# A two-layer encoder on one core: half of the second attention's probability tiles transposed on VectorE and through DRAM, and the softmax factor multiplied into the gate

## The chip, the core and the metric

The kernel runs on one core of a Trainium2 chip. The core has five engines that run their own instruction lists in order: PE (TensorE, matrix multiplication; the profile lists its weight loads apart, as PEld), DVE (VectorE), ACT (ScalarE), POOL (GpSimd) and SP (SyncE), which here issues all DMAs. Matrix products land in PSUM, eight banks of 128 x 512 floats, and DVE or ACT carries them to SBUF. POOL works on SBUF only. The metric is the device time of one execution in microseconds, and lower is better.

## The reference

The program is two encoder layers over 1024 tokens of width 1024. The first uses differential attention, the second multi-head latent attention; the change is in the second.

```python
def _mla(h, positions, w_in, q_a_norm_g, w_q_b, kv_a_norm_g, w_kv_b, w_out):
    proj = h @ w_in
    q_a, c_kv, k_pe, z = jnp.split(proj, [384, 640, 704], axis=-1)
    q = (_rmsnorm(q_a, q_a_norm_g) @ w_q_b).reshape(b, s, 8, 128 + 64)
    q_nope, q_pe = q[..., :128], _rope(q[..., 128:], positions)
    k_pe = _rope(k_pe[:, :, None, :], positions)[:, :, 0]
    kv = (_rmsnorm(c_kv, kv_a_norm_g) @ w_kv_b).reshape(b, s, 8, 128 + 128)
    k_nope, v = kv[..., :128], kv[..., 128:]
    # for each block of 128 queries
    sc = (einsum('bqhd,bkhd->bhqk', qn, k_nope) + einsum('bqhr,bkr->bhqk', qp, k_pe)) * 192 ** -0.5
    p = jax.nn.softmax(sc, axis=-1)
    o = einsum('bhqk,bkhd->bqhd', p, v)
    return (o.reshape(b, s, 1024) * jax.nn.silu(z)) @ w_out
```

There are eight heads, so the second attention has 8 x 8 = 64 blocks of 128 queries against 1024 keys.

## The kernel before

**Stages.** The program runs the first layer's projections, its attention, its output projection, then the second layer's projections, its attention (`attn1`, L1710, called for heads 0 to 6 at L1780 and for the last head at L1815) and its output projection. All matrix products take each operand as a high part and a low part (what rounding to the `fp32r` form leaves over), and multiply high x high, high x low and low x high (`mm3`, L186 to L188).

**One block of scores.** `scores1` (L1687) makes the scores of 128 queries against 1024 keys, a tile `s` of two PSUM banks, out of ten products of 512 columns (L1703). There are two such tiles (`sc=2`), so the block after next needs the first one's tile back. `softmax_part` (L401) takes the row maximum on DVE (L404) and the exponential on ACT (L406), which reads `s` and writes `e` to SBUF together with the row sum in `zz`. The factor 1/sum is not applied there.

**Transposing.** The second product needs the probabilities with the keys on the partitions. `transpose_p` (L382) does half a block: four transposes of 128 x 128 on PE (L387) into the one bank `tr`, then ACT copies the bank to the high part `pth` (L389), then DVE subtracts that from the bank into the low part `ptl` (L390). The bank is free for the next half when DVE is through. A block has two halves, in `Tail.turn(0)` and `turn(1)`.

**The second product.** Two blocks make a pair. `Tail.pv` (L987) multiplies the pair's `pth` and `ptl` with the head's values `vt` into the bank `pv`: 12 products of 256 columns for each half of the keys, 24 for the pair. Two pairs fill the bank (a half of the 1024 queries). `close` in `attn1` then multiplies the bank with the gate `gz` on DVE (L1721), and `finish` (L910) inverts `zz` (L1722), spreads it over the partitions by a DMA to DRAM and back (`bc_d`, `bc_s`), multiplies it in on POOL (L916), splits the result into high and low (L921, L922) and stores both (`oS`).

**The order.** Python code names the order by hand, and a build step may move an instruction on its own engine where its inputs stand late in that step's plan; what stands then is fixed. For block n, `scores1` issues its ten products with `turn(1)` of block n-2 after the sixth. `after_scores` (L1019) issues `turn(0)` of block n-1, and behind each second block the second product of the pair before. Between these stand steps of a stream of other products, the projections of the next heads' queries and keys (`FILL1`, L42: how many steps at which of four places; one step is three products `acc` of 512 columns). The SP queue issues the DMAs in its own order, and a DMA that waits holds all behind it. The values of a head are two tiles `vt` of 512 KB out of three buffers.

The last head is called with no stream steps, and works on the output projection's first products (`oacc`) instead.

Of the kernel before, what the change touches and what calls it, by code (L numbers as in the profile page):

```python
# [21 lines left out]
P = 128  # L22
D = 1024
# [18 lines left out]
FILL1 = ((1, 0, 1, 0), (0, 1, 0, 0)) * 4  # L42
# [28 lines left out]
HL_V = (0, 1)  # L71
Q_CHUNK = 6
# [19 lines left out]
def trunk(ctx: ExitStack, tc: tile.TileContext, A, out):  # L92
# [303 lines left out]
    def alloc_pt(ap_):  # L396
        pth = [ap_.tile([P, 4, 2 * P], F32R, name="pth", tag="pt", bufs=6) for _ in range(2)]
        ptl = [ap_.tile([P, 4, 2 * P], F32R, name="ptl", tag="pt", bufs=6) for _ in range(2)]
        return pth, ptl
# [510 lines left out]
    def finish(o, y, l, h, half, dst, ap_, dgs):  # L910

        if dst is None:
            b, rb = bcast_rows(ap_, y, "osq", 4)
# [60 lines left out]
    class Tail:  # L974
# [12 lines left out]
        def pv(self, kh):  # L987
            c, qp = self.c, self.qp
            if self.t == 0:
                return  # L990
            if kh == 0:
                if qp == 0:
                    c["vt"] = load_v(c["pool"], c["l"], c["h"])
                if qp % 2 == 0:
                    c["o_"] = bank("pv", "pv")
                    c["open"](qp // 2)
            cs = slice((qp % 2) * 256, (qp % 2) * 256 + 256)
            pv(c["o_"][:, cs], c["vt"], *self.pt, kh)
            if kh == 1 and qp % 2 == 1:
                c["close"](qp // 2, c["o_"], self.zz)  # L1000

    tails, hooks = [None, None], []

# [15 lines left out]
    def after_scores(fill, n):  # L1019

        prev, last = tails
        if last:
            last.turn(0)
        fill(n)
        if prev:
            prev.pv(0)
        fill(n + 1)
        new = hooks[:]
        if prev:
            prev.pv(1)  # L1030
        fill(n + 2)
        for f in new:
            hooks.remove(f)
            f()

    def attn0(h, fills, extra=None, late=None):
# [10 lines left out]
        ctx_ = dict(pool=a0b, l=0, h=h, open=lambda half: None, close=close)  # L1047
        for qp in range(4):
            half = qp // 2
            if qp % 2 == 0:  # L1050
                zz = first.pop(0) if first else sm.tile([P, 4], F32, name="zz")
            for t in range(2):
# [13 lines left out]
                if first:  # L1066
                    e0 = first.pop()
                else:
                    e0 = q_tile(h, half, (qp * 2 + t) % 4, zz, a0b, mid)
                    fill(2)  # L1070
                    after_scores(fill, 3)
                side.tick()
                tails[:] = [tails[1], Tail(qp, t, e0, zz, ctx_)]
# [171 lines left out]
    tail0 = attn0(NH - 1, lambda i: FILL7[i] if i < Z_LAST else (0,) * 6, extra0, late0)  # L1245
    mk.clear()
# [30 lines left out]
    def group0(gi, fulls):  # L1277
# [3 lines left out]
        def chunk(k):  # L1281
            if gi == 1:
                h1[k][1] = xt2k("h1h"), xt2k("h1l")
                h1f[k] = ut(f"h1f{k}", dt=F32)
# [19 lines left out]
    def ut(name, spare=False, dt=F32R):  # L1304
        return up.tile([P, HF], dt, name=name, tag="us" if spare else "u", bufs=4 if spare else 20)
# [4 lines left out]
    wp = pool(stw, "wp1", side="right")  # L1310
    stv = ExitStack()
# [31 lines left out]
    def combos():  # L1343
# [5 lines left out]
        for k in range(4):  # L1349
# [19 lines left out]
            split_t(3, k, t3_, (ut("t3h"), ut("t3l")))  # L1369
# [228 lines left out]
    cqput = lora(3, CQ, qag, QL, lambda: ut("cqr", dt=F32), lambda: ut("cq"), 1)  # L1598
# [4 lines left out]
    def gate_steps():  # L1603
# [14 lines left out]
        for j in range(KT):  # L1618
# [6 lines left out]
            for i in range(2):  # L1625
                with behind("V"):
# [60 lines left out]
    def scores1(h, half, ti, zz):  # L1687
# [18 lines left out]
        return softmax_part(ap, s_ps, zz[:, ti : ti + 1])  # L1706
# [3 lines left out]
    def attn1(h, fills, extra=None, late=None):  # L1710

        def open_(half):
            ctx_["gz"] = wst.tile([P, HF], F32, name="gz1", tag="gz", bufs=3)
            SP.dma_start(ctx_["gz"], zS[h, half])

        def close(half, o_, zz):
            if late and half == 1:
                ctx_["late"] = late(o_, zz, ctx_["gz"])
                return
            o = ap2.tile([P, HF], F32, name="o1", tag="o", bufs=2)  # L1720
            V.scalar_tensor_tensor(out=o, in0=o_, scalar=0.5, in1=ctx_["gz"], op0=ALU.mult, op1=ALU.mult)  # L1721
            V.reciprocal(zz, zz)  # L1722
            finish(o, zz, 1, h, half, None, ap2, None)

        ctx_ = dict(pool=ap, l=1, h=h, open=open_, close=close)
        for qp in range(4):
            half = qp // 2
            if qp % 2 == 0:
                zz = first1.pop(0) if first1 else sm.tile([P, 4], F32, name="zz1")
            for t in range(2):  # L1730
# [7 lines left out]
                if first1:  # L1738
# [207 lines left out]
```

## Time and profile before

| | us |
|---|---|
| median of three runs | 1428.52 (1428.01 to 1430.89) |
| the profiled execution | 1429.47 |
| its span on the core | 1427.7 |
| PE busy in the span | 1396.7 |
| DVE / ACT / POOL busy | 903.3 / 743.3 / 603.7 |
| the stretch 1040 to 1290 us, in the second attention: PE / DVE / ACT / POOL busy | 249.6 / 145.3 / 129.0 / 67.8 of 250 |

The span leaves out 1.8 us of the profiled execution's own time. A row of a group reads: line, engine, operation, out<-in by the program's names, shapes and count, then busy time and mean duration of one in ns, then how long the engine stood idle just before these instructions and what ended it. Products on PE are pipelined: the profile shows one of 512 columns as about 0.39 us long, while the next one starts 0.23 us after it. So a busy share of PE counts overlap once and can't be divided by the mean duration; how long PE needs for a row of products is read from the starts in the timeline.

### The profile page before, as it was taken

Reading aid. Unit: us, or ns where it says so; the run is one execution under the profiler, and the core shown is the slowest. Engines: PE = TensorE matmul, PEld = TensorE weight load, DVE = VectorE, ACT = ScalarE, POOL = GpSimd, SP = SyncE. Lnnn points to the kernel's source line nnn. Section 1 sums busy time; section 2 is a strip of 40 time slices with the busy share of each in tenths; the row PEclk is TensorE's granted clock in tenths of the full one; section 3 lists DMA queues with packets and bytes.
Section 4 is the critical chain, followed back from the end, with each engine's and each line's share of the span. In section 5 each row is a group of like instructions: output and inputs, shape, how many; then the busy total and the mean of one; then the engine's idle time right before and its main releaser. Section 6 shows DMA issues by size and latency. Waiting matters only on the chain.

```text
span 1427.7 us, 20748 instructions
## 1 busy us (share of the span) xinstructions
PE 1396.7 (98%) x7478; PEld 1167.8 (82%) x7478; DVE 903.3 (63%) x1366; ACT 743.3 (52%) x1318; POOL 603.7 (42%) x483
## 2 busy tenths in 40 slices
PE   9999899999999999998999999999999999999997
PEld 7778688888888887887788788887888888888886
DVE  7756786767777767677435876255566555555355
ACT  6623375666565656566343644345455454555442
POOL 4415164656464646453561244412241331413562
PEclk9999999999999999999999999999999999999999
DMA  9777723233332333236663132465334532336663
GB/s 350 252 231 231 243 69 95 84 103 82 96 98 88 94 92 89 89 96 224 240 200 125 52 104 82 146 191 167 113 115 115 135 101 81 99 96 215 217 209 138
DMA packets 128473, 201.64 MB, mean 141 GB/s; under 512 B 17777, under 2 KB 54769, under 8 KB 128370
## 3 DMA queue, kind: packets, MB, share of 16 engines
q1 hardware_dynamic: 128370, 200.31, 45.6%
q8 instruction: 59, 0.97, 0.3%
q14 instruction: 44, 0.36, 0.1%
HBM read 131.11 MB, written 45.55 MB: 124 GB/s over the span
## 4 chain that ended last, share of the span: by engine, by line
PE 80%; DVE 6%; DMA 5%; issue 3%; ACT 3%; POOL 2%; SPq 1%; ACTq 0%; POOLq 0%; DVEq 0%
PE s L1703 9%; PE acc L188 8%; PE acc L186 8%; PE acc L187 8%; PE tr L387 7%; PE s L873 7%; PE oacc L186 4%; PE oacc L188 4%; PE oacc L187 4%; PE pv L187 4%; PE pv L188 4%; PE pv L186 4%; DVE ada L444 2%; PE zacc L186 1%; PE zacc L188 1%
## 5 line engine op out<-in xcount | busy, mean ns | idle before, releaser
L389 ACT CAST pth<-tr 128x512 fp32r<-128x512 f32 x256 | 150.2, 587 | 280.4 <-PE tr L387 277.2
L404 DVE TENSOR_REDUCE nm<-s 128x1 f32<-128x1024 f32 x192 | 233.9, 1219 | 72.7 <-PE s L873 66.3
L390 DVE TENSOR_TENSOR ptl<-tr,pth 128x512 fp32r<-128x512 f32 x256 | 176.1, 688 | 136.6 <-ACT pth L389 136.1
L235 POOL TENSOR_TENSOR wl<-wraw,wh 128x512 fp32r<-128x512 f32 (+2 forms) x82 | 101.3, 1237 | 234.6 <-ACT wh L234 212.5
L387 PE MATMUL tr<-ident,e 128*128 128x128 f32 x1024 | 154.6, 273 | 4.4 <-DVE ptl L390 4.2
L387 PEld LDWEIGHTS tr<-ident,e 128*128 128x128 f32 x1024 | 120.7, 140 | 46.1 <-DVE ptl L390 22.6
L406 ACT ACTIVATE e<-s,nm 128x1024 f32<-128x1024 f32 x128 | 143.6, 1122 | 24.8 <-DVE nm L404 24.4
L186 PE MATMUL acc<-h0h,wh 128*128 128x512 f32 x360 | 151.2, 420 | 2.5 <-DVE v_hl L366 1.7
L186 PE MATMUL pv<-pth,vt 128*128 128x256 f32 x512 | 147.4, 288 | 0.0
L187 PE MATMUL pv<-ptl,vt 128*128 128x256 f32 x512 | 145.8, 285 | 0.0
L188 PE MATMUL pv<-pth,vt 128*128 128x256 f32 x512 | 144.7, 283 | 0.0
L188 PE MATMUL acc<-h0h,wl 128*128 128x512 f32 x360 | 142.9, 397 | 0.1
L187 PE MATMUL acc<-h0l,wh 128*128 128x512 f32 x360 | 142.0, 394 | 0.0
L1118 POOL TENSOR_TENSOR wol<-wor,woh 128x512 fp32r<-128x512 f32 x64 | 84.7, 1343 | 83.7 <-ACT woh L1117 79.5
L186 PEld LDWEIGHTS pv<-pth,vt 128*128 128x128 f32 x512 | 97.3, 190 | 3.1 <-ACT pth L389 0.5
L187 PEld LDWEIGHTS pv<-ptl,vt 128*128 128x128 f32 x512 | 97.5, 190 | 2.8
L188 PEld LDWEIGHTS pv<-pth,vt 128*128 128x128 f32 x512 | 97.7, 191 | 0.1
L873 PE MATMUL s<-ks,qa 128*128 128x512 f32 x256 | 82.7, 403 | 5.2 <-DVE e L881 2.7
L336 POOL TENSOR_TENSOR rp_sw<-rp_sw,sinT 128x512 f32<-128x512 f32 x42 | 55.3, 1316 | 71.1 <-DMA rp_sw<-rp_raw 69.5
L881 DVE SCALAR_TENSOR_TENSOR e<-s,z,e 128x1024 f32<-128x1024 f32 x64 | 82.1, 1283 | 2.1
L331 POOL TENSOR_TENSOR rp_r<-rp_raw,cosT 128x512 f32<-128x512 f32 x38 | 49.7, 1307 | 77.3 <-ACT rp_raw L326 44.0
L873 PE MATMUL s<-ks,qb 128*128 128x512 f32 x256 | 81.1, 396 | 0.5 <-DMA qb<-qb 0.5
(624 smaller groups left out, 3355.5 us busy)
## 6 DMA issues: line engine op xcount, KB each, us to landing
ada<-in_ada_ss SPq DMA_DIRECT2D x32, 512.0 KB, 6.8
wraw<-in_w_s SPq DMA_DIRECT2D x64, 256.0 KB, 2.8
vS<-v_hl SPq DMA_DIRECT2D x32, 512.0 KB, 4.8
vt<-vS SPq DMA_DIRECT2D x32, 512.0 KB, 4.5
wor<-in_w_out SPq DMA_DIRECT2D x64, 256.0 KB, 3.5
rp_sw<-rp_raw SPq DMA_DIRECT2D x168, 64.0 KB, 2.0
bc_s<-bc_d SPq DMA_DIRECT2D x30, 256.0 KB, 4.2
oS<-bc_s SPq DMA_DIRECT2D x30, 256.0 KB, 2.6
```

The costliest lines, as they stand in the source:

```text
L186: PE.matmul(psum, ah, bh, start=first, stop=False)
L187: PE.matmul(psum, ah, bl, start=False, stop=False)
L188: return PE.matmul(psum, al, bh, start=False, stop=last).ins
L235: sub = (lo_on or (V if pair_of else G)).tensor_sub(l_[:, :n], raw[:, :n], f32v(h_[:, :n]))
L387: PE.transpose(tr[:, j, :], p[:, kt * P : (kt + 1) * P], ident)
L389: mk["S"] = S.copy(pth[kh][:, :, dst], tr).ins
L390: mk["V"] = V.tensor_sub(ptl[kh][:, :, dst], tr, f32v(pth[kh][:, :, dst])).ins
L404: mk["V"] = V.reduce_max(nm, s_ps, axis=AX.X, negate=True).ins
L406: mk["S"] = S.activation(e, s_ps, AF.Exp, bias=nm, scale=1.0, accum_out=zs).ins
L873: PE.matmul(s_ps[:, kc * HF : (kc + 1) * HF], src[:, c, ql], KS[h][kc][:, c, :], start=fst, stop=not fst)
L1118: in_turn(G.tensor_sub(lo, raw, f32v(hi)))
L1703: PE.matmul(s_ps[:, kc * HF : (kc + 1) * HF], lhs, rhs(kc), start=i == 0, stop=i == 4)
```

## The change

In heads 0 to 6 of the second attention, the first pair of each half (blocks 0, 1 and 4, 5 of the eight) is no longer transposed on PE. Its `e` tile goes through a new class `Mate`: `move` lets DVE transpose all its 32 x 32 pieces into `eT` (128 x 1024) and stores that in DRAM (`pS`, 512 KB a block); `fetch`, two blocks after the pair's second block, reads the pair back with the pieces in their places (`pr`, four DMAs of 256 KB, in runs of 256 floats); `split`, two blocks later, makes `pth` on ACT (two copies of 128 x 1024) and `ptl` on DVE (128 x 1024) and POOL (two of 128 x 512); the pair's second product is due two blocks after that, so behind that of the pair that follows it. The other pair of each half and the whole last head are transposed on PE as before.

Beside that: the factor 1/sum is multiplied into the gate tile `gz` before the second product ends (`factor`: inverse on DVE, `bc_d` and `bc_s` by DMA, the multiplication on POOL, one block after another), so that `close` multiplies bank and gate and splits at once. The stores `oS` go out two blocks later. `vt` is loaded at a block set by `settle`. `FILL1` puts its stream steps at other places, with the same number in all. `e` of the second attention has two buffers in place of three, `pt` eight in place of six. The tiles of the second values' projection take other buffers, and a part of the pool `u` becomes a pool `ub` that is closed earlier. Up to the projection of the second values, the same instructions stand in the same order on every engine.

```diff
-FILL1 = ((1, 0, 1, 0), (0, 1, 0, 0)) * 4
+FILL1 = ((1, 1, 0, 0), (0, 0, 1, 0), (1, 1, 0, 0), (0, 0, 1, 0)) * 2
+SPLIT_AT = 4
+PV_AT = 6
+FACTOR_AT = (1, 2, 3)
...
+    class Mate(Tail):
+        def __init__(self, qp, c):
+            self.qp, self.t, self.c, self.zz = qp, 1, c, c["zz"]
+            self.store = dr.tile([2, P, D], F32, name="pS", tag="pS", bufs=3)
+
+        def move(self, t, e):
+            eT = self.c["pool"].tile([P, D], F32, name="eT", tag="eT", bufs=self.c["nT"])
+            mk["V"] = V.transpose(eT.rearrange("p (c k j) -> p c k j", c=4, j=32), e.rearrange("p (k c i) -> p c k i", c=4, i=32)).ins
+            mk["SP"] = SP.dma_start(self.store[t], eT).ins
+
+        def fetch(self):
+            self.raw = self.c["pool"].tile([P, 2, 4, 256], F32, name="pr", tag="pr", bufs=1)
+            src = self.store.rearrange("t (a i) (c r) -> c i t a r", a=4, c=4)
+            for c_ in range(4):
+                mk["SP"] = SP.dma_start(self.raw[c_ * 32 : c_ * 32 + 32], src[c_]).ins
+
+        def split(self):
+            pth, ptl = self.pt = alloc_pt(self.c["pool"])
+            r = self.raw.rearrange("p t a (k j) -> p k (t a) j", j=32)
...
+            for kh in range(2):
+                S.copy(view(pth[kh]), r[:, kh * 4 : kh * 4 + 4])
+            for kh, a, b, eng in ((0, 0, 4, V), (1, 0, 2, G), (1, 2, 4, G)):
+                eng.tensor_sub(view(ptl[kh][:, a:b]), r[:, kh * 4 + a : kh * 4 + b], view(f32v(pth[kh][:, a:b])))
...
+    def settle(e, tail, mate, t, qp, ctx_, late):
+        n = now[0]
...
+        if t and qp == 0:
+            prep.setdefault(n + (1 if late else 3), []).append(load)
+        if mate:
+            mate.move(t, e)
+            if t:
+                prep.setdefault(n + 2, []).append(mate.fetch)
+                prep.setdefault(n + SPLIT_AT, []).append(mate.split)
+                due.setdefault(n + PV_AT, []).extend([lambda: mate.pv(0), lambda: mate.pv(1)])
+        elif t and not (late and qp == 3):
+            due.setdefault(n + (3 if late and qp == 0 else 2), []).extend([lambda: tail.pv(0), lambda: tail.pv(1)])
...
-        return softmax_part(ap, s_ps, zz[:, ti : ti + 1])
+        return softmax_part(ap, s_ps, zz[:, ti : ti + 1], 2)
...
+            def out_():
+                V.reciprocal(zz, zz)
+                SP.dma_start(d_.rearrange("(p t) -> p t", p=P), zz)
+            def in_():
+                with behind("SP"):
+                    SP.dma_start(b, d_[None, :].to_broadcast([P, HF]))
+            def mul():
+                in_turn(G.tensor_mul(t3(gz), t3(gz), b.rearrange("p (q t) -> p t q", t=4)))
+            for i, f in enumerate((out_, in_, mul)):
+                prep.setdefault(n + FACTOR_AT[i], []).append(f)
...
+            def split():
+                with behind("S"):
+                    S.copy(b.bitcast(F32R), o)
+                in_turn(G.tensor_sub(o.bitcast(F32R), o, b))
+                prep.setdefault(now[0] + 2, []).append(put)
...
+            mate = Mate(qp, ctx_) if qp % 2 == 0 and not late else None
...
-            v1_tile(tt, 1, ap, "pt", 6)
+            v1_tile(tt, 1, ap, *V1_BUF[tt % 5])
```

What this does to the order, at three places. The numbers behind the names tell one buffer's use from another's. The first place is PE's row between two blocks of a middle head before: the last four products of block `s1_11980`, three stream products, and a transposed half on either side (`tr_11987` of one block, `tr_12012` of the next).

```order
L387 MATMUL tr_11987<-ident_79,e_11887 128x128 x4
L1703 MATMUL s1_11980<-kps0_7101,qpa_11292 128x512
L1703 MATMUL s1_11980<-kps1_7102,qpa_11292 128x512
L1703 MATMUL s1_11980<-kps0_7101,qpb_11293 128x512
L1703 MATMUL s1_11980<-kps1_7102,qpb_11293 128x512
L186 MATMUL acc_12002<-ck_8757,wh_11794 128x512
L187 MATMUL acc_12002<-ck_8758,wh_11794 128x512
L188 MATMUL acc_12002<-ck_8757,wl_11795 128x512
L387 MATMUL tr_12012<-ident_79,e_11928 128x128 x4
```

Seven products stand between two uses of the bank `tr`. Now, on PE at the start of a middle head, behind 48 products of the bank `pv_11712` (two pairs in a row, of which the last three are shown):

```order
L190 MATMUL pv_11712<-pth_11678,vt_11622 128x256
L191 MATMUL pv_11712<-ptl_11680,vt_11622 128x256
L192 MATMUL pv_11712<-pth_11678,vt_11622 128x256
L391 MATMUL tr_11848<-ident_79,e_11756 128x128 x4
L391 MATMUL tr_11876<-ident_79,e_11787 128x128 x4
L1776 MATMUL s1_11959<-kn_h_11444,qn_h_11654 128x512
L1776 MATMUL s1_11959<-kn_h_11543,qn_h_11654 128x512
```

The two halves, of two blocks, stand back to back, and the next block's scores behind them. In the whole second attention the bank is now used 72 times in place of 128.

The second place is PE's row from the end of a block to the start of the block after next, which takes the same tile `s`. Before, a whole block, two transposed halves and a pair's second product or stream products stood between. Now, in a middle head (`s1_11557` ends, `s1_11626` has six of its ten, `s1_11687` is the block after next):

```order
L1776 MATMUL s1_11557<-kps1_7102,qpb_11181 128x512
L391 MATMUL tr_11576<-ident_79,e_11538 128x128 x4
L1776 MATMUL s1_11626<-kn_h_10893,qn_h_11397 128x512
L1776 MATMUL s1_11626<-kn_h_10965,qn_h_11397 128x512
L1776 MATMUL s1_11626<-kn_l_10894,qn_h_11397 128x512
L1776 MATMUL s1_11626<-kn_l_10966,qn_h_11397 128x512
L1776 MATMUL s1_11626<-kn_h_10893,qn_l_11398 128x512
L1776 MATMUL s1_11626<-kn_h_10965,qn_l_11398 128x512
L190 MATMUL acc_11665<-cq_9404,wh_11504 128x512
L191 MATMUL acc_11665<-cq_9405,wh_11504 128x512
L1776 MATMUL s1_11687<-kn_h_10893,qn_h_11397 128x512
```

Nine rows of work have stayed between the two; the rest of `s1_11626` and the second product come later. The third place is DVE's row in a middle head, before:

```order
L404 TENSOR_REDUCE nm_11998<-s1_11980 128x1
L390 TENSOR_TENSOR ptl_11932<-tr_12012,pth_11930 128x4x128
L1643 TENSOR_TENSOR kn_l_12023<-acc_12002,kn_h_12022 128x512
L390 TENSOR_TENSOR ptl_11933<-tr_12033,pth_11931 128x4x128
L404 TENSOR_REDUCE nm_12044<-s1_12026 128x1
L390 TENSOR_TENSOR ptl_12050<-tr_12052,pth_12048 128x4x128
L1721 SCALAR_TENSOR_TENSOR o1_12087<-pv_11948,gz1_11949 128x512
L390 TENSOR_TENSOR ptl_12051<-tr_12101,pth_12049 128x4x128
L404 TENSOR_REDUCE nm_12112<-s1_12094 128x1
```

and now, from the second block of one such pair to the first of the next:

```order
L1018 STREAM_TRANSPOSE eT_12161<-e_12159 128x1024
L394 TENSOR_TENSOR ptl_12012<-tr_12146,pth_12010 128x4x128
L408 TENSOR_REDUCE nm_12208<-s1_12197 128x1
L1724 SCALAR_TENSOR_TENSOR qn_l_12219<-acc_12177,qn_h_12218 128x512
L408 TENSOR_REDUCE nm_12238<-s1_12227 128x1
L1799 RECIPROCAL zz1_12061<-zz1_12061 128x4
L1724 SCALAR_TENSOR_TENSOR qn_l_12311<-acc_12265,qn_h_12310 128x512
L1037 TENSOR_TENSOR ptl_12131<-pr_11989,pth_12129 128x1024
L394 TENSOR_TENSOR ptl_12244<-tr_12246,pth_12242 128x4x128
L394 TENSOR_TENSOR ptl_12245<-tr_12325,pth_12243 128x4x128
L408 TENSOR_REDUCE nm_12336<-s1_12318 128x1
```

The row maximum of `s1_12318` stands behind the subtraction of the fetched pair (`pr_11989`), which waits for a DMA, and behind two evictions of the bank `tr`.

More of the change, by code (lines that the diff above doesn't have):

```diff
@@ L1004, in run_tails, with after_scores @@
+    def after_scores(fill, i):
+        if tails[1]:
+            tails[1].turn(0)
+        fill(i)
+        new = hooks[:]
+        todo_ = due.pop(now[0], [])
+        for j in range(max(2, len(todo_))):
+            if todo_:
+                todo_.pop(0)()
+            if j < 2:
+                fill(i + 1 + j)
+        for f in new:
+            hooks.remove(f)
+            f()
     def run_tails(fill):
@@ L1815, in trunk @@
     tail1 = attn1(NH - 1, lambda i: (0, 0, 0, 0), extra1, late1)
+    assert not prep and not due
     mk.clear()
```

131 lines of the change are left out of this document (82 added, 49 removed).

## The prediction

> **What bounds the kernel now.** I read the page first: the span, the busy shares, the slices and the chain that ended last.
>
> ```profile
> span 1427.7 us, 20748 instructions
> ...
> PE 1396.7 (98%) x7478; PEld 1167.8 (82%) x7478; DVE 903.3 (63%) x1366; ACT 743.3 (52%) x1318; POOL 603.7 (42%) x483
> ...
> PE 80%; DVE 6%; DMA 5%; issue 3%; ACT 3%; POOL 2%; SPq 1%; ACTq 0%; POOLq 0%; DVEq 0%
> PE s L1703 9%; PE acc L188 8%; PE acc L186 8%; PE acc L187 8%; PE tr L387 7%; PE s L873 7%; PE oacc L186 4%; PE oacc L188 4%; PE oacc L187 4%; PE pv L187 4%; PE pv L188 4%; PE pv L186 4%; DVE ada L444 2%; PE zacc L186 1%; PE zacc L188 1%
> ```
>
> PE is busy nearly always and makes 80% of the chain. The changed operations lie in the second attention, so I cut that stage out by windows (columns: busy time and count on PE, PEld, DVE, ACT, POOL; granted clock, DMA share, GB/s), and group its instructions.
>
> ```profile
> 1000.00:1040.00 40.00, 38.26 (x234) 32.76 (x233) 22.07 (x34) 19.82 (x37) 12.94 (x10) 1.00 0.41 116
> 1040.00:1290.00 250.00, 249.60 (x1516) 214.14 (x1515) 145.31 (x205) 128.95 (x235) 67.81 (x54) 1.00 0.38 109
> ```
>
> ```profile
> L390 DVE TENSOR_TENSOR ptl<-tr,pth 128x512 fp32r<-128x512 f32 x88 | 60.7, 689 | 73.8 <-ACT pth L389 73.4
> L404 DVE TENSOR_REDUCE nm<-s 128x1 f32<-128x1024 f32 x44 | 53.5, 1215 | 4.9 <-PE s L1703 4.9
> L387 PE MATMUL tr<-ident,e 128*128 128x128 f32 x348 | 52.4, 273 | 0.4 <-DVE ptl L390 0.4
> L389 ACT CAST pth<-tr 128x512 fp32r<-128x512 f32 x88 | 51.7, 587 | 102.9 <-PE tr L387 102.6
> L406 ACT ACTIVATE e<-s,nm 128x1024 f32<-128x1024 f32 x44 | 49.5, 1125 | 2.7 <-DVE nm L404 2.6
> ...
> L916 POOL TENSOR_TENSOR o<-o,bc_s 128x512 f32<-128x512 f32 x11 | 17.0, 1546 | 24.7 <-DVE o L1721 23.1 <-DMA bc_s<-bc_d 1.6
> ```
>
> In 250 us PE stands idle for 0.4; the others have 42% of their time or more free, at full clock. PE alone sets this stage, and what leaves it is won until another wait takes its place. The 44 blocks and 11 closed halves of the window make 5.5 heads, 45.5 us each.
>
> **What a transposed half costs PE.** Not its 273 ns times four, since products overlap; the starts tell (start and duration in us, from the timelines of PE, DVE, PEld and ACT).
>
> ```profile
> 1158.67 0.62 PE L1703 MATMUL s<-kn_h,qn_l 128*128 128x512 f32 x2
> 1159.13 0.60 PE L387 MATMUL tr<-ident,e 128*128 128x128 f32 x4
> 1159.48 0.71 PE L1703 MATMUL s<-kps,qpa 128*128 128x512 f32 x2
> ...
> 1160.38 0.69 DVE L390 TENSOR_TENSOR ptl<-tr,pth 128x512 fp32r<-128x512 f32 x1
> 1160.99 1.21 DVE L404 TENSOR_REDUCE nm<-s 128x1 f32<-128x1024 f32 x1
> ...
> 1161.13 0.42 PEld L387 LDWEIGHTS tr<-ident,e 128*128 128x128 f32 x4 [0.23 <-DVE ptl L390]
> ...
> 1162.31 1.12 ACT L406 ACTIVATE e<-s,nm 128x1024 f32<-128x1024 f32 x1
> 1163.32 0.20 ACT L406 ACTIVATION_READ_ACCUMULATOR e<-s,nm 128x1 f32 x1
> ```
>
> Two products of 512 columns advance PE by 1159.13 - 1158.67 = 0.46 us, so 0.23 each. The four transposes advance it by 1159.48 - 1159.13 = 0.35 us. Two chains stand in the same rows. The bank `tr` is free again, and the next weights load, at 1161.13: 2.00 us after the first transpose, so PE needs 1.65 us of other work between two halves. A tile `s` is free after maximum and exponential: 1.21, a gap of 0.11, then from 1162.31 to 1163.52, in all 2.53 us, or about 2.7 with the handover on either side (an estimate).
>
> **The change, part by part.**
>
> *Removed from PE.* The bank is used 72 times in place of 128, so 56 halves go: 56 x 0.35 = 19.6 us. All of it lies on the path, as PE has no idle time to lose it in.
>
> *Waits on the bank `tr`.* In the new order three pairs of halves stand back to back (1.65 us each), one pair has two products between (1.65 - 0.46 = 1.2) and two have five (1.65 - 1.15 = 0.5 each): 5.0 + 1.2 + 1.0 = 7.2 us. Before, seven products (1.6 us) stood between, and the row shows 0.4 us lost in all. It is less, down to 0, only where PE would have waited there for something else anyway, and more, up to another 1.2 us a place (7 us), where a DVE transpose stands ahead of the subtraction. I take 7.2.
>
> *Waits on the tiles `s`.* By the same steps I add up PE's work between a block's end and the start of the block after next. Before it was 3.0 us or more at every block, mostly 8.3. Now 16 distances are under 4 us, six of them under 2.7: three of 2.19, one of 2.54, two of 2.64. With nothing else on DVE and ACT, the chain of 2.7 us costs 3 x 0.5 + 0.2 + 2 x 0.1 = 1.9 us. If one DVE transpose of 1.2 us stands ahead of the maximum at all 16, the chain is 3.9, and what the distances lack of it adds up to 12 us. I take a third of that, 4 us, because only half of the blocks are transposed on DVE and not every transpose meets a maximum.
>
> *Added on DVE.* No row shows the 32 x 32 transpose. One pass over 1024 elements is 1.215 us by the row of L404; two passes would be 2.43. A gain is excluded, as it is a new instruction. I take 1.2, since the work reads and writes each element once. The subtraction of 128 x 1024 has both inputs in SBUF; the nearest rows are of L1338, where such a subtraction of half the size either runs alone or is held up (shown as min/median/max):
>
> ```profile
> L1338 DVE TENSOR_TENSOR t4l<-t4f,t4h x4: 679/692/1809, 808.6 to 834.0; 128x512 fp32r<-128x512 f32 x4
> L1338 DVE TENSOR_TENSOR t3l<-t,t3h x4: 678/680/691, 810.3 to 835.5; 128x512 fp32r<-128x512 f32 x4
> ```
>
> So it takes from 1.2 us (as L404) to 1.2 + 1.13 held up. Per head DVE had 145.3 / 5.5 = 26.4 us; eight evictions go (5.5), four transposes and two subtractions come (7.3 to 14.4): 28.2 to 35.3 us of some 43. It is no new bound by load, and its cost is the delay taken above. [...]
>
> *ACT and POOL.* ACT loses eight casts of 0.587 (4.7 us a head) and gets four of twice the size, at the exponential's 1.125 each: 4.5. POOL gets four subtractions of 128 x 512, at most 1.55 each as in L916, 6.2 us on 67.8 / 5.5 = 12.3. The factor's multiplication is the same one on another tile. Cover for all three is their own idle time: 0. If that cover went, two casts in a row would hold an exponential by 2.3 us.
>
> *Added on the DMA queue.* Each head stores 4 x 512 KB and fetches 2 x 1 MB, 4.2 MB more.
>
> ```profile
> DMA packets 16059, 27.35 MB, mean 109 GB/s; under 512 B 3781, under 2 KB 5061, under 8 KB 16041
> ...
> q1 hardware_dynamic: 16041, 27.11, 37.7%
> ...
> vt<-vS SPq DMA_DIRECT2D x10, 512.0 KB, 4.2
> ...
> bc_s<-bc_d SPq DMA_DIRECT2D x11, 256.0 KB, 3.8
> ```
>
> ```profile
> DMA packets 17954, 16.16 MB, mean 162 GB/s; under 512 B 1278, under 2 KB 14334, under 8 KB 17946
> ...
> q1 hardware_dynamic: 17946, 16.06, 56.6%
> ...
> vS<-v_hl SPq DMA_DIRECT2D x12, 512.0 KB, 6.4
> ```
>
> The first fence is of 1040 to 1290 us: 0.377 x 250 / 27.11 = 3.5 us of all engines per MB. The second is of 940 to 1040 us, where packets averaged 900 bytes: 0.566 x 100 / 16.06 = 3.5 again, so runs of 1 KB should cost no more. The share becomes (17.1 + 14.6) / 43 = 74%, from 38%. A store lands in 4.2 to 6.4 us. A fetch lands between 3.7 us (all at rate) and 15.2 (four times 3.8, one after another); I take 6. Two blocks, 10.7 us, stand before the fetch, two more before the split, and two more before the product. It is covered: 0. On SP a waiting fetch holds the next `vt`, `gz` and the halves of `qpa`, which the next head's scores wait for; that is what costs if the cover goes.
>
> *The rest* (buffers, `FILL1`, the order of the values' projection) removes no work. Where it is hidden PE's neighbours hide it; at 1000 to 1040 us PE has 1.7 us idle, so it may gain or lose that much; I take 0. Earlier stages keep their order.
>
> **The sum.** -19.6 + 7.2 + 4 = -8.4 us. Against the profiled execution's own 1429.47 (its span of 1427.7 and 1.8 around it) that is 1421.1. The median shown, 1428.52, is 0.95 lower: 1420.1, and I predict 1420.
>
> **The rivals.**
>
> *Everything is hidden.* The bank's waits fall where data would have been late anyway, the chain of `s` keeps up: -19.6, at best 1409. For it speaks the free time on DVE, against it the back-to-back halves. Chance 0.13.
>
> *All is given back.* The tiles `s` cost the 12 us of the upper end: -19.6 + 7.2 + 12 = -0.4, so 1428. Chance 0.14.
>
> *VectorE holds the scores (slower).* If a transpose takes two passes, the chain behind one is 2.7 + 2.4 = 5.1 us, and 32 distances are shorter than that; what they lack adds up to 40 us: -19.6 + 7.2 + 40 = +27.6, at most 1456. It decides from 12.4 us of such delay, so where a third of this falls on PE. For it speaks that DVE's row is fixed, with maxima behind transposes and held subtractions; against it, that its load stays below 83%. Chance 0.18.
>
> *The fetch is late (slower).* At 15.2 us for 10.7, ACT and DVE stand 4.5 us behind each of 14 fetches, 63 us; with the 12 us that are won else it decides from 0.9 us a fetch. Against it speak the 3.5 us per MB at 900 bytes. Chance 0.04. [...]
>
> That the transposes stay on PE is excluded by the order.
>
> **How the numbers follow.** My forecast, 1413 to 1425, gets 0.51. About 0.2% (2.9 us) is what a measurement of this kernel can tell from no change. Faster: 0.51 + 0.13 and a little of the case between, 0.65. Same: 0.14. Slower: 0.21, of which the upper half, above 1438, is left out of the range, with little below 1409. The range is 1409 to 1438.
>
> **What would show it.** Right: `tr` under L391 with 56 halves fewer; PE idle of about 7 us ended by `ptl`; idle before `s` of a few us ended by the exponential; the transpose near 1.2 us; fetches landing within 10 us. Wrong: a transpose above 2 us; DVE or ACT idle ended by the DMA `pr`; PE idle before `s` for `qpa` or before `pv` for `vt`.

## The result: slower, and the profile after

| | before | after |
|---|---|---|
| median, us | 1429.54 (1428.01 to 1430.89, 4 runs) | 1444.25 (1443.21 to 1448.69, 4 runs) |
| ratio | | 1.0109, 95% interval 1.0085 to 1.0134 |
| the profiled execution, its span | 1429.47, 1427.7 | 1448.69, 1446.9 |

The forecast was 1420 us, its range ended at 1438; the change costs 15 us. The page of after (span; busy times; the chain that ended last):

```profile
span 1446.9 us, 20472 instructions
...
PE 1388.4 (96%) x7254; PEld 1157.9 (80%) x7254; DVE 925.9 (64%) x1352; ACT 741.0 (51%) x1290; POOL 650.8 (45%) x511
...
PE 69%; issue 7%; DVE 7%; DMA 6%; POOL 4%; ACT 4%; SPq 2%; POOLq 0%; ACTq 0%; DVEq 0%
```

PE has 224 products fewer (56 halves of four) and is busy 8 us less, but its share of the chain fell from 80% to 69%, and POOL's rose to 4%. The second attention by windows, first of before, then of after (columns as in the prediction):

```profile
1000.00:1345.00 345.00, 342.87 (x2088) 294.62 (x2087) 194.43 (x277) 175.94 (x320) 101.93 (x78) 1.00 0.43 126
```

```profile
1040.00:1290.00 250.00, 227.09 (x1248) 192.19 (x1246) 153.22 (x184) 120.23 (x203) 100.77 (x75) 0.97 0.71 193
1000.00:1345.00 345.00, 315.51 (x1772) 267.28 (x1771) 209.09 (x252) 168.28 (x283) 138.00 (x100) 0.97 0.68 191
```

PE idles 345 - 315.5 = 29.5 us where it idled 2.1, and its granted clock is 0.97 where it was 1.00, an estimated 345 x 0.03 = 10 us. Over the whole span the clock is 0.987 for 0.997, an estimated 14 us. Together these nearly close the account: 24.6 us of products gone (not the 19.6 reckoned, as the part on the prediction shows), 27.4 of idle time come, 14 of lower clock: +17, where the two spans differ by 19. What ended the idle time (PE's waits, 1000 to 1345 us; total us, times, longest), before:

```profile
PE tr L387 <- DVE ptl L390: 2.1, 3, 1.4
```

and after:

```profile
PE tr L391 <- DVE ptl L394: 11.1, 8, 3.8
PE acc L192 <- POOL wl L239: 10.2, 7, 3.5
PE s L1776 <- ACT e L410: 4.0, 6, 2.0
PE pv L191 <- DVE ptl L1037: 3.2, 2, 2.3
PE pv L191 <- POOL ptl L1037: 0.8, 2, 0.4
```

The second row had no place in the sum at all: the low parts `wl` of the projection stream's weights, made on POOL. The new operations themselves cost about what was reckoned (groups over the whole run):

```profile
L1037 POOL TENSOR_TENSOR ptl<-pr,pth 128x512 fp32r<-128x512 f32 x28 | 43.5, 1576 | 138.0 <-ACT pth L1035 119.3 <-issue 18.6
L1018 DVE STREAM_TRANSPOSE eT<-e 128x1024 f32<-128x1024 f32 x28 | 34.7, 1240 | 11.5 <-ACT e L410 11.0
L1035 ACT CAST pth<-pr 128x1024 fp32r<-128x1024 f32 x28 | 28.0, 1046 | 0.0
L1037 DVE TENSOR_TENSOR ptl<-pr,pth 128x1024 fp32r<-128x1024 f32 x14 | 21.7, 1547 | 2.8 <-ACT pth L1035 2.5 <-DMA rp_sw<-rp_raw 0.2
```

The DVE transpose takes 1.24 us (reckoned 1.2), and ACT never waits for the fetched data (0.0). Each of the four DMAs of a fetch lands 4.8 us after its issue on the median; from the first issue to the last landing the four take 7.3 us (reckoned 6; the median of the seven fetches whose landings are all in the trace). 71% of the DMA engines' time is used, from 1040 to 1290 us:

```profile
q1 hardware_dynamic: 29984, 48.08, 70.8%
...
pr<-pS SPq DMA_DIRECT2D x43, 256.0 KB, 4.8
pS<-eT SPq DMA_DIRECT2D x21, 512.0 KB, 4.7
```

So every new operation is about as cheap as hoped, no fetched data is late for ACT, and PE waits all the same. One place shows how (timelines of PE, ACT, DVE, POOL and SP of after):

```profile
1176.03 0.73 PE L1776 MATMUL s<-kn_h,qn_h 128*128 128x512 f32 x2 [0.34 <-ACT e L410]
...
1182.43 0.79 PE L192 MATMUL acc<-cq,wl 128*128 128x512 f32 x1 [3.47 <-POOL wl L239]
...
1170.13 0.50 ACT L238 CAST wh<-wraw 128x384 fp32r<-128x384 f32 x1
...
1174.77 1.11 ACT L410 ACTIVATE e<-s,nm 128x1024 f32<-128x1024 f32 x1 [2.25 <-DVE nm L408]
1175.78 0.19 ACT L410 ACTIVATION_READ_ACCUMULATOR e<-s,nm 128x1 f32 x1
1175.88 1.99 ACT L1035 CAST pth<-pr 128x1024 fp32r<-128x1024 f32 x2
...
1173.45 1.23 DVE L408 TENSOR_REDUCE nm<-s 128x1 f32<-128x1024 f32 x1 [0.50 <-PE s L1776]
...
1177.94 3.04 POOL L1037 TENSOR_TENSOR ptl<-pr,pth 128x512 fp32r<-128x512 f32 x2 [8.98 <-ACT pth L1035]
1180.94 1.44 POOL L239 TENSOR_TENSOR wl<-wraw,wh 128x384 fp32r<-128x384 f32 x1
...
1175.92 0.51 SPq L1834 DMA_DIRECT2D oS<-o  x1
1181.00 1.80 SPq L1025 DMA_DIRECT2D pr<-pS  x4
1182.85 0.45 SPq L1794 DMA_DIRECT2D gz<-zS  x1
```

ACT had `wh` ready at 1170.63, so POOL could have made `wl` in the 7.3 us that it then still stood idle. But its row has the fetched pair's subtractions first. These wait for ACT's casts, which stand behind an exponential, which waits for a row maximum, which waits for PE's scores. PE then stands 3.5 us for `wl`. An idle engine is no cover when the row's next instruction waits. And SP's next fetch, which its row reaches at 1176.4, stands until 1181.0, when POOL lets go of the single buffer `pr`; `gz` and all else on SP stand behind it. The clock by windows, just then:

```profile
1180.00:1184.00 4.00, 1.57 (x6) 1.47 (x7) 1.53 (x2) 0.00 (x0) 3.88 (x3) 0.64 0.48 114
1184.00:1188.00 4.00, 4.00 (x18) 3.71 (x17) 0.00 (x0) 0.00 (x0) 0.00 (x0) 0.50 1.10 212
```

Behind the gap PE is granted half its clock, 0.50 for 6.8 us (from 1181.2 us on): a second price of the same wait.

### The profile page after: what moved, and what is told of

Same layout as the page of the kernel before. It is cut to its first block, busy times and chain, and to the rows that moved or that the text cites. A ratio compares the mean times of both kernels' runs of the same rounds, so it can differ in the third digit from the quotient of the medians.

```text
span 1446.9 us, 20472 instructions
## 1 busy us (share of the span) xinstructions
PE 1388.4 (96%) x7254; PEld 1157.9 (80%) x7254; DVE 925.9 (64%) x1352; ACT 741.0 (51%) x1290; POOL 650.8 (45%) x511
## 4 chain that ended last, share of the span: by engine, by line
PE 69%; issue 7%; DVE 7%; DMA 6%; POOL 4%; ACT 4%; SPq 2%; POOLq 0%; ACTq 0%; DVEq 0%
PE acc L192 8%; PE acc L190 8%; PE acc L191 8%; PE s L877 7%; PE s L1776 5%; PE tr L391 5%; PE oacc L190 4%; PE oacc L192 4%; PE oacc L191 4%; PE pv L191 3%; PE pv L192 3%; PE pv L190 3%; DVE ada L448 2%; POOL ptl L1037 1%; PE zacc L190 1%
## 5 line engine op out<-in xcount | busy, mean ns | idle before, releaser
L393 ACT CAST pth<-tr 128x512 fp32r<-128x512 f32 x200 | 117.4, 587 | 250.9 <-PE tr L391 242.9
L394 DVE TENSOR_TENSOR ptl<-tr,pth 128x512 fp32r<-128x512 f32 x200 | 136.9, 685 | 84.2 <-ACT pth L393 84.1
L391 PE MATMUL tr<-ident,e 128*128 128x128 f32 x800 | 122.3, 275 | 13.9 <-DVE ptl L394 13.7
L391 PEld LDWEIGHTS tr<-ident,e 128*128 128x128 f32 x800 | 96.5, 141 | 44.3 <-DVE ptl L394 20.2
L1037 POOL TENSOR_TENSOR ptl<-pr,pth 128x512 fp32r<-128x512 f32 x28 | 43.5, 1576 | 138.0 <-ACT pth L1035 119.3
L190 PEld LDWEIGHTS pv<-pth,vt 128*128 128x128 f32 x512 | 99.2, 194 | 5.1 <-ACT pth L393 1.6
L192 PEld LDWEIGHTS pv<-pth,vt 128*128 128x128 f32 x512 | 99.8, 195 | 0.3
```

The lines of the kernel that those rows point to most:

```text
L190: PE.matmul(psum, ah, bh, start=first, stop=False)
L192: return PE.matmul(psum, al, bh, start=False, stop=last).ins
L391: PE.transpose(tr[:, j, :], p[:, kt * P : (kt + 1) * P], ident)
L393: mk["S"] = S.copy(pth[kh][:, :, dst], tr).ins
L394: mk["V"] = V.tensor_sub(ptl[kh][:, :, dst], tr, f32v(pth[kh][:, :, dst])).ins
```

## The experiments

All ran beside the kernel before (1429.0 to 1430.5 us in these). "Idle" is PE's waiting by the starts of its products between 990 and 1345 us (before 2.6, after 34.2). "Short" counts, in PE's built row, the blocks of scores that start less than 4 us of PE's work behind the last use of their tile `s`, as in the prediction (before 2, after 16); many mean a bunched order.

| run | edit against after | us | ratio to before (95%) | idle | short |
|---|---|---|---|---|---|
| e1 | low parts of pairs on DVE | 1432.7 | 1.0019 (1.0008 to 1.0031) | 23.7 | 15 |
| e2 | stream's `wl` on DVE | 1436.6 | 1.0047 (1.0034 to 1.0061) | 26.1 | 14 |
| e4 | no trip through DRAM | 1406.1 | 0.9826 (0.9804 to 0.9849) | 3.7 | 2 |
| e10 | trip of 1/32 of the bytes | 1404.5 | 0.9828 (0.9800 to 0.9855) | 3.7 | 2 |
| e7 | all bytes, no reader, SP's queue | 1433.5 | 1.0027 (1.0014 to 1.0040) | 26.1 | 12 |
| e11 | the same, POOL's queue | 1407.8 | 0.9843 (0.9826 to 0.9859) | 1.9 | 2 |
| e5 | no pair through DRAM | 1435.4 | 1.0030 (1.0017 to 1.0043) | 6.4 | 2 |
| e17 | e5, factor behind PV | 1438.1 | 1.0054 (1.0036 to 1.0072) | 6.3 | 2 |
| e18 | e17, old strip table | 1433.6 | 1.0033 (1.0020 to 1.0046) | 6.0 | 2 |
| e8 | PV one block later | 1456.0 | 1.0171 (1.0141 to 1.0202) | 38.6 | 12 |
| e9 | e8, low parts on DVE | 1436.4 | 1.0036 (1.0021 to 1.0052) | 20.9 | 11 |
| e12 | fetch from POOL's queue | 1430.1 | 0.9997 (0.9978 to 1.0016) | 18.9 | 2 |
| e13 | fetch from ACT's queue | 1456.4 | 1.0188 (1.0158 to 1.0217) | 37.4 | 2 |
| e14 | e12, split and PV a block later | 1419.7 | 0.9925 (0.9904 to 0.9946) | 14.9 | 4 |
| e15 | e14, low parts on DVE | 1429.2 | 0.9989 (0.9975 to 1.0002) | 21.9 | 3 |
| e16 | e12, low parts on DVE | 1423.4 | 0.9956 (0.9939 to 0.9974) | 18.4 | 2 |
| e19 | e14, fetch a block earlier | 1413.8 | 0.9888 (0.9867 to 0.9910) | 11.6 | 4 |
| e20 | e19, fetch from SP's queue | 1455.9 | 1.0196 (1.0155 to 1.0237) | 41.6 | 13 |

### POOL's and DVE's rows (e1, e2)

```diff
 # e1
-            for kh, a, b, eng in ((0, 0, 4, V), (1, 0, 2, G), (1, 2, 4, G)):
+            for kh, a, b, eng in ((0, 0, 4, V), (1, 0, 4, V)):
 # e2, in gen_strips, called with lo_on=V for stream1
-                        for a, b in zip(nxt, split_raw(*raws.pop(0))):
+                        for a, b in zip(nxt, split_raw(*raws.pop(0), lo_on=lo_on)):
```

> The fetched pair's low parts are all subtracted on DVE (two of 128 x 1024), none on POOL. Theory A (the split's subtractions stand on the in-order rows of POOL and DVE ahead of work that PE waits for): PE's wait of 11 us for the stream's low weights on POOL goes, the subtraction on DVE is no longer held up by POOL (1.23 us each in place of 2.3), so about 1435 us. Theory B (the extra 29 MB through DRAM make data late): nothing changes, 1444. Theory C (the fixed order on PE itself, halves back to back and blocks too close): 1444, with the waits moved to other places.

> The stream's low weight parts are subtracted on DVE in place of POOL; the split stays as in the changed kernel. Theory A: PE's 11 us wait for them on POOL goes, DVE has 2 to 3 us more a head, so 1433 to 1437 us. Theory B: 1444. Theory C: 1444 or slower, since DVE gets more work ahead of the row maxima.

Both regain a part, 11.6 and 7.6 us. In e1 the wait for `wl` is down to 0.5 us, but 12.3 us of waits of `tr` for DVE stay. So POOL's row is a cause, worth about the 10.2 us of that wait, and not the whole.

### The trip: work, waiting, bytes, queue (e4, e10, e7, e11)

e4 splits `eT` where the DVE transpose left it, with no store and no fetch, so the output differs from the reference's; all other work stays. The pair then shares one tile `eT` with two buffers, and the single buffer `pr` is gone; both hold for e7, e10 and e11 too.

```diff
 # e4
-            mk["SP"] = SP.dma_start(self.store[t], eT).ins
 # e10: as e4, but with
+            mk["SP"] = SP.dma_start(self.store[t], eT[:, 0:32]).ins
+                mk["SP"] = SP.dma_start(self.raw[c_ * 32 : c_ * 32 + 32, :, :, 0:8], src[c_]).ins
 # e7: as e4, but with the whole store, and fetched into a DRAM tile that nothing reads
+                mk["SP"] = SP.dma_start(ghost[c_ * 32 : c_ * 32 + 32], src[c_]).ins
 # e11: the last line with POOL's queue
+                G.dma_start(ghost[c_ * 32 : c_ * 32 + 32], src[c_])
```

> The pair's transposed pieces are split straight from SBUF, without the store to DRAM and the fetch, so the pieces of the probabilities are at wrong places and the output differs; all instructions of PE, ACT, DVE and POOL remain. Theory B: the loss goes, 1420 us or less. Theory A and C: 1440 to 1446, since ACT never stood idle for the fetch in the trace.

> The reverse: the split reads the block where the transpose left it, as in the kernel without the trip (the output differs), but a thirty-second of the store and of the fetch stays (32 of 1024 columns stored, four fetches of 8 columns written into a corner of the block), so that each split still waits for a store and a fetch, with hardly any bytes. Theory W (waiting for the trip): 1420 us or more, since the two latencies in a row stay. Theory T (bytes): 1405 to 1410 us.

> The kernel without the trip (the probabilities are split where the transpose left them, so the output differs), but with the trip's traffic put back with nobody waiting for it: each transposed block is stored as before and read again with the same 1 KB runs, into a DRAM tile that nothing uses. Theory T (it is the traffic: loads of weights, V and gates land late behind it, and the build, which reckons with that, hands out an irregular order): most of the loss is back, 1422 to 1440 us. Theory W (it is the waiting of the split for its own data): nothing waits, so 1405 to 1410 us, as without any trip.

> The traffic without a reader again (store and idle fetch; the output differs), only the fetches are issued from POOL's queue in place of SP's. The bytes are the same, but the build now hands out a regular order on TensorE (deficit in bank tr 0.4 us for 5.7; 2 rows of scores under 4 us apart for 12). Theory O (the loss comes from the order that the build hands out, since it reckons that everything behind the fetch on SP's queue lands late): 1404 to 1412 us. Theory T (the bytes slow the chip itself): 1425 to 1436 us, as from SP's queue. If issuing from POOL's queue is dear, POOL's row shows it and the stream waits for its low parts.

Without the trip the kernel gains 24 us, more than the 19.6 that the removed products were reckoned at: DVE's transposes, ACT's casts and the subtractions on DVE and POOL are all in e4 and fit beside PE. Waiting for a store and a fetch in a row costs nothing either (e10). The bytes do, from SP's queue (e7: +27 us over e4), and do not from POOL's (e11: +2). PE's waits of e7:

```profile
PE acc L192 <- POOL wl L239: 11.4, 6, 3.9
PE tr L391 <- DVE ptl L394: 6.3, 7, 1.4
PE s L1778 <- ACT e L410: 1.8, 3, 0.9
```

and of e11, between 1000 and 1330 us:

```profile
PE tr L391 <- DVE ptl L394: 1.2, 1, 1.2
PE s L1778 <- ACT e L410: 0.4, 1, 0.4
```

Two of the same waits as in after, though nobody reads what e7 fetches; the queue takes them away, with the DMA engines' share no lower (0.75 in e11 for 0.65 in e7, from 1040 to 1290 us). So it is not DMA bandwidth. What differs is SP's row, and with it the row that the build lays on PE: in e7 it puts three pairs of halves back to back (PE waits 1.40 us between the halves of each) and has 12 short distances; in e11 there are no such pairs and 2 short distances, from code that differs in the queue alone. Late data has a part in e7 as well: between 1000 and 1345 us POOL waits 27.6 us there for `bc_s` and 18.8 for `rp_sw`, both fetched on SP's queue (15.9 and 3.2 in e11), and one of PE's three long waits for `wl`, of 2.5 us, stands behind such a wait. In after POOL's waits for a DMA come to 2.6 us.

### The other parts of the change (e5, e17, e18)

```diff
 # e5 (FACTOR_AT becomes (1, 1, 2))
-            mate = Mate(qp, ctx_) if qp % 2 == 0 and not late else None
+            mate = None
 # e17: and close() goes back to
+            V.reciprocal(zz, zz)
+            finish(o, zz, 1, h, half, None, ap2, None)
 # e18: and
+FILL1 = ((1, 0, 1, 0), (0, 1, 0, 0)) * 4
```

> All pairs are transposed on PE again; the factor in the gate, the buffers, the places of the stream steps and the settle logic stay (the factor one block earlier, as the products come earlier). If the loss comes from these other parts: 1436 us or more. Theory A, B and C: 1427 to 1432, with PE without gaps again.

> No block goes through DRAM, and the softmax factor is applied behind PV as before; what is left of the change is the strip table, the buffers and the time of the V loads. With the factor in the gate this was 1435 us, 5 us over before. If the factor costs it: 1429 to 1431 us; if the table and buffers: 1434 to 1436 us.

> No block through DRAM, factor behind PV, and the strip table FILL1 of before; of the change only buffers and the time of the V loads stay. If the strip table cost the 5 to 8 us of the kernel without mates and factor (its order on TensorE has 23 short distances in bank tr, 3.0 us in all, for 0.4 with the old table): 1429 to 1432 us. If buffers and V loads: 1435 to 1439 us.

Where all pairs stay on PE, what the change has beside the trip costs 5 us, and not for the factor: without it the kernel is no faster. The strip table accounts for 4.5 us of the 8 there (without mates; with them it has other work to fill). The 4.6 us that stay in e18, buffers and the time of the V loads, were not taken apart.

### One block later on SP's queue (e8, e9)

```diff
-PV_AT = 6
+PV_AT = 7
```

> The full change with one number moved: the products with V of a pair that went through DRAM come one block of scores later (PV_AT 7 for 6). The order on TensorE is then regular again: nowhere two halves back to back in bank tr (deficit 0.5 us for 7.4), the rows of scores under 4 us apart 12 for 16 and none under 2.6. Theory O (the built order is what costs): the waits tr, s and pv fall from 22 us to under 8, the wait of the projection stream for POOL's low parts (11 us) stays, 1428 to 1434 us. Theory T in its narrow form (late landings on the chip itself): 1440 to 1447 us, with TensorE still waiting in the same places.

> The same with all low parts of a fetched pair on VectorE, so that POOL's row holds only the stream's and the factor's work. Theory O: the wait for the stream's weights goes too, waits under 10 us in all, 1414 to 1424 us. If VectorE becomes what holds the scores, as a rival had it, waits before s and tr rise again: 1430 us or more. Theory T: 1432 us as with VectorE's low parts alone, or more.

A miss. The back-to-back halves were gone from PE's row, yet e8 is 12 us slower than after. `tr` still waits 11.9 us, now mainly in four waits of 2.1 to 3.8 us at other places, and `wl` costs 15.5; the granted clock is 0.94 between 1000 and 1345 us for 0.97 in after, by estimate 10 of the 12 us. So a regular row on PE is not enough: other waits took the place of the halves', and these end with DVE's and POOL's work. In e9 the waits for `wl` are gone; `tr` waits 14.2 us for DVE.

### The fetch on another queue (e12 to e16, e19, e20)

```diff
 # e12 (e13: S.dma_start)
-                mk["SP"] = SP.dma_start(self.raw[c_ * 32 : c_ * 32 + 32], src[c_]).ins
+                G.dma_start(self.raw[c_ * 32 : c_ * 32 + 32], src[c_])
 # e14: as e12, and
-SPLIT_AT = 4
-PV_AT = 6
+SPLIT_AT = 5
+PV_AT = 7
 # e15, e16: as e14, as e12, with the line of e1
 # e19: as e14, and
-                prep.setdefault(n + 2, []).append(mate.fetch)
+                prep.setdefault(n + 1, []).append(mate.fetch)
 # e20: as e19, with SP.dma_start
```

> The full change with all its waits and bytes and the right output; the four fetches of a pair are issued from POOL's queue in place of SP's. Order on TensorE regular (deficit 0.4 us for 7.4, 2 rows of scores under 4 us apart for 16). Theory O: 1406 to 1416 us, faster than before by 1% or more; theory T: 1430 us or more; a price of POOL's issuing (56 more instructions in its row) would lie between, 1416 to 1428.

> The full change with the fetches issued from ScalarE's queue. The order on TensorE lies between (deficit in bank tr 4.9 us, but 2 rows of scores under 4 us apart). Theory O: 1410 to 1422 us; theory T: 1430 us or more. ScalarE is 51% busy, so that 56 issues in its row should cost it nothing that TensorE sees.

e12 regains 14 us, less than hoped: data now really is late, where it never was from SP's queue (ACT's and PE's waits of e12):

```profile
ACT pth L1035 <- DMA pr<-pS: 15.8, 6, 3.7
...
PE pv L190 <- DMA vt<-vS: 3.3, 1, 3.3
```

ACT's queue is the wrong one (e13): a fetch that waits there stands ahead of casts and exponentials, and PE waits 13.4 us before `pv` for ACT's casts.

> Fetches from POOL's queue, and one block of scores more between the fetch and the split, and so before the products with V (SPLIT_AT 5, PV_AT 7). Theory L (the data lands later on the chip than the order allows): ScalarE's 16 us of waiting for fetched data nearly go, and the wait before pv with them: 1412 to 1420 us. Theory R (POOL's row, now with 56 issues more, holds the stream's low parts): 1424 to 1430 us, with 8 us of waiting for them still there.

> As e14, and all low parts of a fetched pair on VectorE. If both theories hold a part, this is the fastest with the right output: 1408 to 1416 us, TensorE waiting under 8 us between 990 and 1345 us. If VectorE then holds the scores: 1420 us or more, with waits before tr and s.

> Fetches from POOL's queue, the old slack, all low parts of a fetched pair on VectorE. Theory R: the 8 us before the stream's low parts go, 1416 to 1423 us. Theory L: the data is as late as before, and now on VectorE's row, which TensorE waits for: 1428 us or more.

One block more of room regains 10 us (e14), so lateness was a part. Low parts on DVE gain 7 us at the old distance (e16 against e12) and cost 9 at the new one (e15 against e14). In both PE then waits some 12 us before `tr` for ACT's exponentials (12.3 and 12.0), which stand behind DVE's row of maxima and subtractions, two of 128 x 1024 a pair at 1.67 and 1.85 us each on the mean. In e16 that replaces other waits (e12 had 7.8 us for `wl` and 3.3 for `vt`); in e15 little was left to replace.

> The fastest version (fetches on POOL's queue, one block of slack more) with each fetch asked for one block earlier in the program. If the fetch on POOL's row is late because of its place in the program: ScalarE's 11 us of waiting for fetched data fall under 4 us, 1413 to 1418 us. If that wait lies beside TensorE's work or comes from the stores: 1418 to 1423 us, no change.

> The fastest version (1414 us: fetch one block earlier, SPLIT_AT 5, PV_AT 7), with its fetches on SP's queue again as in the change. If slack and early fetch do it: 1412 to 1420 us. If it is the queue (13 rows of scores under 4 us apart in the built order, one at 1.0, for 4 from POOL's queue): 1430 us or more, with TensorE waiting over 20 us between 990 and 1345 us.

e19 is the fastest kernel with the whole computation, 1.1% faster than before and 2.1% than after. Its page, and PE's waits between 1000 and 1330 us:

```profile
PE 1373.4 (97%) x7254; PEld 1147.9 (81%) x7254; DVE 924.9 (65%) x1352; ACT 742.4 (53%) x1290; POOL 683.8 (48%) x567
```

```profile
PE tr L391 <- DVE ptl L394: 6.4, 7, 1.9
PE tr L391 <- ACT e L410: 3.0, 2, 1.6
PE pv L190 <- DMA vt<-vS: 0.6, 1, 0.6
```

The time came as expected, the reason did not: ACT still waits 14.6 us for fetched data (11.0 in e14), and PE does not see it; gone are the waits for `wl` and nearly all for `vt`. e20 has the same program with the fetches on SP's queue and takes 42 us more: slack and early fetch are worth nothing there. Its waits:

```profile
PE acc L192 <- POOL wl L239: 13.1, 5, 3.6
PE tr L391 <- DVE ptl L394: 11.4, 9, 2.3
PE pv L191 <- DVE ptl L1037: 3.7, 2, 2.8
```

and SP's row, where the fetches stand for DVE and POOL to let go of `pr`, up to 10.4 us, and the halves of `qpa` for ACT:

```profile
SPq L365 <- ACT qpa L360: 41.5, 6, 10.4
SPq L1025 <- DVE ptl L1037: 34.1, 6, 10.4
```

## Why the prediction was wrong

*Right in kind, too small: the removed products (19.6 us).* The row behind the prediction's 1159.48 in before, and the page of e4:

```profile
1160.03 0.62 PE L1703 MATMUL s<-kps,qpb 128*128 128x512 f32 x2
...
PE 1372.5 (98%) x7254; PEld 1148.3 (82%) x7254; DVE 918.2 (65%) x1352; ACT 739.9 (53%) x1290; POOL 650.5 (46%) x511
```

The two products behind a transposed half advance PE by 1160.03 - 1159.48 = 0.55 us, not by 0.46; so a half costs 0.35 + 0.09 = 0.44 us (the medians over 86 halves of before say the same), and 56 of them 24.6 us. In e4, with all the new work on DVE, ACT and POOL in place, PE is busy 24.2 us less than before, and e4 and e10 gain 24 to 25 us. The change lost its 15 us in spite of a gain that was 5 us larger than reckoned.

*Right: the new operations.* Transpose 1.24 for 1.2 us; the subtraction on DVE 1.55 us on the mean, within its bounds of 1.2 to 2.33; on POOL 1.58 for 1.55; a whole fetch 7.3 for 6 us, DMA share 71% for 74%. The slow rival by a two-pass transpose fell with this: its sign came true, its mechanism did not.

*Right in size, in part by luck: the waits on `s`,* 4 for 4.0 us, half of it at one place (2.0). *Too small: those on `tr`,* 7.2 for 11.1 us (9 more than before). The places that were counted came out nearly right, 6.9 us: PE waits 1.40 us between the halves of each of the three back-to-back pairs (reckoned 1.65), 2.18 where two products stand between (1.2), and 0.24 where five do (0.5 each). What was missed is 4.2 us at two other places, 3.8 of it here (DVE and PE of after):

```profile
1053.61 1.22 DVE L408 TENSOR_REDUCE nm<-s 128x1 f32<-128x1024 f32 x1 [1.51 <-PE s L1776]
1054.76 2.31 DVE L1037 TENSOR_TENSOR ptl<-pr,pth 128x1024 fp32r<-128x1024 f32 x1
1056.99 0.68 DVE L394 TENSOR_TENSOR ptl<-tr,pth 128x512 fp32r<-128x512 f32 x1
...
1057.82 0.68 PE L391 MATMUL tr<-ident,e 128*128 128x128 f32 x4 [3.79 <-DVE ptl L394]
```

The bank `tr` was ready for DVE's eviction when ACT's cast of it ended, at 1052.66. But the fetched pair's subtraction stands ahead of the eviction in DVE's row, behind a maximum that waits for scores, and takes its upper bound of 2.3 us. The prediction named a DVE transpose ahead of the eviction, 1.2 us, and not this subtraction.

*Wrong: "Cover for all three is their own idle time: 0".* This is the step that failed first. POOL idles more than half of the time (busy 45% of the span), and PE waited 10.2 us for it, because its low parts of the stream stand in a row behind subtractions that wait. e1 takes them apart and regains 11.6 us. The waits before `pv`, 4.0 us, were put at 0 in the same way. At 1182 us, and in the 3.8 us before `tr` above, what PE waits for stands behind the fetched pair's subtractions; before `pv` it is one of them.

*Wrong: "It is covered: 0", of the trip.* The data does come in time, which was all that was asked. The text named the danger, a waiting fetch on SP that holds what is behind it, and gave it no price. e7 and e11, and then e19 and e20, price SP's queue, by whatever way it acts, at 26 and 42 us. A fetch waits on SP mostly until the pair before is split, as `pr` has one buffer (in after 55.8 us in all for DVE and POOL between 1000 and 1330 us), and little for its store (5.2 us). e7 has no such wait for a buffer and loses 26 us against e11 too, so that the buffer alone is not the cause.

*Not priced: the clock.* About 10 us of after in the second attention, by the estimate above; most of the other 4 us lies in earlier stages, whose order did not change. In e19 and e11 the granted clock is 1.00 from 1000 to 1345 us.

*Not refuted: "The rest", 0.* Strip table and buffers cost some 5 us where all pairs stay on PE (e5). But e4, e10 and e11 have them too and gain 22.7 to 25 us, nearly the whole of the products, so that with half of the pairs gone from PE little of it is left.

These prices overlap and are not added: the account that nearly closes is the one by products, waits and clock in the first section.

What stays open: whether SP's queue does its harm by what stands behind it on the chip, or by the rows that the build lays out when it plans around SP. Both change together in e7 and e11, and in e19 and e20. For the rows speaks that in after all engines but SP wait for DMAs by 2.8 us in all between 1000 and 1345 us; for the chip, that POOL in e7 waits for late data, as said above. Since e8 is slow without back-to-back halves, and e13 with two short distances, no single count of PE's row suffices. Two buffers for `pr` on SP's queue were not tried.

## What to carry to other kernels

Idle time of an engine covers new work only if nothing urgent stands behind it in that engine's row (here POOL was busy 45% of the span, and PE waited 10.2 us for it): ask of each added instruction what it waits for and who needs the next one, DMA queues included. A transfer that waits (for a buffer, for a store) belongs in a queue whose other entries nobody needs soon, with enough blocks between asking, splitting and using (here 1413.8 us in e19 for 1455.9 from SP's queue in e20). Before a trip through memory is blamed or cleared, run it with the bytes and no reader, and with the reader and no bytes.

## What was not expected of the hardware

*The clock.* In after the granted clock was 0.50 from 1058.3, 1085.6, 1140.2, 1181.2 and 1290.4 us on, for 3.4 us each and once for 6.8, where before it was 1.00 from 1000 to 1345 us. These starts lie whole multiples of 3.41 us apart. Cut after, from 1000 to 1345 us, into stretches on that grid: the five in which PE idled 2.0 to 3.0 us were followed by half clock, and those at full clock in which it idled 1.4 us or less were not (no sharp limit shows: in e12, on its own grid, a stretch with 1.6 us was followed and one with 1.8 was not). So it mattered here how the gaps fell on the grid: from 1300 to 1320 us PE idled 3.8 us in all at 1.00, spread over three stretches. The last of the five, with the stretch behind it:

```profile
1286.96:1290.37 3.41, 1.37 (x9) 0.95 (x8) 3.16 (x4) 2.61 (x5) 0.17 (x1) 1.00 0.37 105
1290.38:1293.78 3.40, 3.40 (x10) 2.64 (x9) 1.41 (x2) 0.66 (x2) 0.00 (x0) 0.50 0.48 172
```

The wait of 3.5 us that ended at 1182.4 cost nearly twice its length: PE worked 5.6 of the 6.8 us at half clock, an estimated 2.8 us more.

*Fetches from POOL's queue took longer.* One DMA took 5.6 us to land there (e19, 1040 to 1290 us) for 4.8 from SP's, and each issue 0.59 us of POOL's row, in which the four of a fetch did not always follow one another: in e19 three were issued from 1113.2 us on and the fourth at 1118.2. A whole fetch took 11.0 us from the first issue to the last landing (12.0 in e12) for 7.3 in after. ACT waits for data in these runs; in e19 PE never waits for the casts of that data.
